# A decoder layer on one core: in its attention stage, the masking and maximum step goes ahead of other work of VectorE

## The chip, the cores and the metric

The kernel runs on one core of one Trainium2 chip, on its own. The metric is the device time of one execution in microseconds (us). Engines are named as in the profile: PE is TensorE (PEld its weight loads), DVE is VectorE, ACT is ScalarE, POOL is GpSimd, and SP is the queue that issues most transfers.

## What is computed

The reference is one layer of a decoder over 512 tokens of width 1024. The input is normalised and projected; one branch pools over windows; the other is a sparse attention with three branches (compressed keys, selected blocks, sliding window) of 16 heads in 2 groups; both are gated, merged and projected, and a squared-ReLU MLP follows. The part that the change touches is the softmax of the selected and the window branch. With 512 tokens there are 8 blocks of 64 keys and up to 16 may be picked, so all causal blocks are picked, and both branches are causal softmaxes over the whole sequence:

```python
def masked_softmax(s, mask):
    s = jnp.where(mask, s.astype(jnp.float32), NEG_INF)
    return jnp.where(mask, jax.nn.softmax(s, axis=-1), 0.0)
...
        s_s = jnp.einsum('bqghd,bgqkd->bghqk', qb, k_sel) * scale
        p_s = masked_softmax(s_s, ok[:, :, None])
        o_s = jnp.einsum('bghqk,bgqkd->bqghd', p_s, v_sel)
...
        s_w = jnp.einsum('bqghd,bkgd->bghqk', qb, kwb) * scale
        p_w = masked_softmax(s_w, wmask)
        o_w = jnp.einsum('bghqk,bkgd->bqghd', p_w, vwb)
        o = gb[..., 0:1] * o_c + gb[..., 1:2] * o_s + gb[..., 2:3] * o_w
```

## The kernel before, in words

Everything is in float32. A weight is split by ACT and DVE into a rounded part and a rest (`wh` on L522, `wl` on L525), and a product is made of three PE products of such parts. The attention stage lies between about 171 and 363 us. Its work is cut into 96 **slots** (`slots`, L1373): 8 pairs of heads, 12 slots to a pair. In the first four slots of a pair (queries 0 to 255) a slot holds both branches, in the other eight (queries 256 to 511) one branch of one head and one block of 128 queries. A slot passes through these steps, each a function:

- `score_pe` (L1387): two PE products (`KH`, `KL`) of 256 to 512 columns into a PSUM bank `psS`. There are three such banks (`S_BANKS`); the scores of the compressed branch, `psC` of `cmp_scores`, take one of the same three at times.
- `smax` (L1408): the step of the change. One DVE instruction for each branch in the slot reads the bank, adds the causal mask, writes the result to a tile `P` in SBUF, and gives each row's extreme to `sm` (a second, short instruction reads the accumulator; the scores are kept negated, so the maximum is taken as a minimum). Once it is done, the bank is free. There are five `P` tiles (`P_BUFS`), so the step of slot i needs the tile of slot i-5, which is free when that slot's transposes are done.
- `expo` (L1425): ACT makes the exponentials in place, with the rows' sums.
- `weight` (L1433): DVE takes reciprocals of the sums (L1440), and POOL multiplies `P` by them and by the gate (L1443).
- `turn_pe`, `turn_hi`, `turn_lo` (L1454, L1469, L1473): PE transposes `P` into a bank `psT` (two of them, `T_BANKS`), ACT copies out the rounded part (L1471) and DVE the rest (L1476). The transposes of slot t need `turn_lo` of slot t-2.
- `pv` (L1478): PE multiplies by the values into the bank `psO`, of which there is one. It begins with two products of the compressed branch (L1485), and these need the bank's last contents taken away by `o_evac` (ACT on L1501, two DVE additions on L1503).

Between these steps PE is given **fillers**: projections of later use (`fill`, `psF` on L566). DVE also splits their weights (L525), does the softmax of the compressed branch (`cmp_scores`, L1336 to L1348) and the rotation of the queries (L905, L948, L949).

The loop at L1518 writes the steps down slot by slot: score of slot i+1, transposes of slot i-4, then `smax` and `expo` of slot i, `weight` of slot i-1, `turn_lo` of slot i-4, and `pv` two slots later (`LAG`, `PLAG`). This is not the order on the engines. A scheduler works through the program as it is built and gives each engine its next instruction by a priority, which by default is the place in the written program; it also gives out the buffers. `tc.high_priority(n)` moves what is written under it n places ahead in this ranking. The order and the buffers are fixed once the program is built, and each engine works through its own list.

Of the kernel before, what the change touches and what calls it, by code (L numbers as in the profile page):

```python
# [62 lines left out]
def trunk(ctx: ExitStack, tc: tile.TileContext, A, out):  # L63
# [519 lines left out]
    def step_side():  # L583
        for _ in range(len(side)):
            g = side.popleft()
            try:
                next(g)
                side.append(g)
            except StopIteration:
                pass  # L590
# [362 lines left out]
    with ExitStack() as c1:  # L953
# [261 lines left out]
        for k in P1[2:]:  # L1215
            i = int(k[-1]) if k[-1].isdigit() else None
# [51 lines left out]
    with ExitStack() as c2:  # L1268
# [46 lines left out]
        def fill(n=1):  # L1315
            for _ in range(n):
                if next(filler, True):
                    return False
                fdone[0] += 1
            return True  # L1320
# [66 lines left out]
        def score_pe(i):  # L1387
            p, half, br, qb, h = slots[i]
            g = p // 4
            nb = qb + 1  # L1390
            ps = ps2.tile([128, S], F32, tag="S", bufs=S_BANKS, name="psS")
            q = Q[p][:, h, 128 * qb:128 * qb + 128]
            for K, a in ((KH[g], True), (KL[g], False)):
                if half == 0:
                    rhs, n = K[:, 0:nb, :, :], 256 * nb
                else:
                    rhs, n = K[:, 0:nb, br, :], 128 * nb
                PE.matmul(ps[:, 0:n], q, rhs, start=a, stop=not a, skip_group_check=True)  # L1398
            live[i] = ps

        def blocks(i):
            p, half, br, qb, h = slots[i]
            nb = qb + 1
            if half == 0:
                return [(b, 128 * nb * b, nb) for b in range(2)]
            return [(br, 0, nb)]

        def smax(i):  # L1408
            p, half, br, qb, h = slots[i]
            ps = live[i]  # L1410
            sm = p2.tile([128, 3, 2], F32, tag="sm", bufs=6, name="sm")
            P = p2.tile([128, S], F32, tag="P", bufs=P_BUFS, name="P")
            for e, (b, o, nb) in enumerate(blocks(i)):
                n = 128 * nb
                if half == 0:
                    s = ps[:, 0:2 * n].rearrange("p (a b c) -> p a b c", b=2, c=128)[:, :, b, :]
                else:
                    s = ps[:, 0:n].rearrange("p (a c) -> p a c", c=128)
                m = cmask[:, S - n:].rearrange("p (a c) -> p a c", c=128)
                DVE.tensor_tensor_reduce(out=P[:, o:o + n].rearrange("p (a c) -> p a c", c=128), in0=s, in1=m,  # L1420
                                         scale=1.0, scalar=3e38, op0=ALU.add, op1=ALU.min,
                                         accum_out=sm[:, 0, e:e + 1])
            live[i] = (ps, sm, P)
# [30 lines left out]
        def turn_pe(i):  # L1454
            p, half, br, qb, h = slots[i]
            ps, sm, P = live[i]
            n = sum(b[2] for b in blocks(i))
            pt = ps2.tile([128, S], F32, tag="T", bufs=T_BANKS, name="psT")
            for j in range(n):
                PE.transpose(pt[:, 128 * j:128 * j + 128], P[:, 128 * j:128 * j + 128], ident)  # L1460
            live[i] = (pt, n)
# [7 lines left out]
        def turn_hi(i):  # L1469
            src, dH, dL = turn_views(i)  # L1470
            his.append(ACT.activation(dH, src, AF.Copy))  # L1471
# [46 lines left out]
        for i in range(n + LAG + PLAG):  # L1518
            if i < n:
                p = slots[i][0]  # L1520
                if i % 12 == 3 and p + 1 < NPAIR:
                    while p + 1 not in Q:
                        fill()
                        step_side()
                if i % 12 == CMP_AT and p + 1 < NPAIR:
                    side.append(cmp_scores(p + 1))
            if i + 1 < n:
                score_pe(i + 1)
                scored["pairs"] = (i + 2) // 12
            t = i - LAG  # L1530
            if 0 <= t < n:
                turn_pe(t)
                turn_hi(t)
            if i < n:
                smax(i)
                expo(i)
            if 0 <= i - 1 < n:
                last = weight(i - 1)
                slot.update(long=i > 3 and slots[i - 1][1] == 1, scaled=last)
            if i > 7 and i % 12 in (0, 2, 4) and len(begun) > 2:  # L1540
                add_sum(last)
            if 0 <= t < n:
                slot["low"] = turn_lo(t)
            step_side()
            want = done0 + (total - done0) * (i + 1) // (n + LAG + PLAG)
            while fdone[0] < want and fill():
                pass
            if i < 5:
                fill()
            if turning:  # L1550
                turn_c()
            j = t - PLAG
            if 0 <= j < n and j % 2 == 1 and pv(j):
                o_evac(*slots[j][0:2])
# [614 lines left out]
```

## Time and profile before

| | |
|---|---|
| time, median of 3 runs | 764.82 us (764.74 to 765.19) |
| profiled execution: its time | 764.3 us |
| its span, first to last instruction | 762.5 us |
| granted clock of TensorE, mean | 0.997 of full speed |
| attention stage, from the timeline | about 171 to 363 us |

The times are of whole executions; the rows of the trace come from the one profiled execution and count from the start of its span. In the timeline a row gives the start, the length, the engine, the line of the kernel, the operation and its tiles, and in square brackets how long the engine was idle just before and what ended that. Buffer numbers are left out there, so a slot is told by its place in the row of slots. Busy time of PE includes the time for which a product's columns run through the array after the next one has begun.

### The profile page before, as it was taken

What the parts mean: (1) busy time and instruction counts of PE and PEld (TensorE: products, weight loads), DVE (VectorE), ACT (ScalarE), POOL (GpSimd) and SP (SyncE); (2) the same over time, 40 slices, a digit from 0 to 9 for tenths busy, and PEclk for the clock granted to TensorE, in tenths of its full rate; (3) what the DMA queues carried; (4) which work ended last, traced back from release to release, by engine and by line L of the source; (5) the groups of instructions that cost most, each with busy time, mean ns of one, the idle gap of its engine ahead of it and who ended that gap; (6) DMA issues with size and microseconds to landing.
All of it is one profiled execution on the core that took longest, in us unless ns stands there. A gap on an engine that the chain in (4) does not pass through costs nothing.

```text
span 762.5 us, 13262 instructions
## 1 busy us (share of the span) xinstructions
PE 752.3 (99%) x4661; PEld 669.7 (88%) x4661; DVE 671.2 (88%) x1282; ACT 513.9 (67%) x978; POOL 190.9 (25%) x271
## 2 busy tenths in 40 slices
PE   9999999999999999999999999999999999999996
PEld 7889999888888888888888899989998999899985
DVE  7998999549988889989689999998899788978897
ACT  7677655339878888898746576944774477447754
POOL 4101010017857767566000020111111111110002
PEclk9999999999999999999999999999999999999998
DMA  9769886864675847343684699989998999798632
GB/s 302 218 187 269 244 239 153 223 188 128 104 195 147 185 106 152 56 112 65 160 294 127 204 289 264 287 218 331 295 267 214 317 299 264 220 302 251 196 110 110
DMA packets 120572, 158.09 MB, mean 207 GB/s; under 512 B 6037, under 2 KB 88505, under 8 KB 120250
## 3 DMA queue, kind: packets, MB, share of 16 engines
q1 hardware_dynamic: 98346, 127.62, 51.5%
q0 software_dynamic: 21872, 28.84, 24.1%
q10 hardware_dynamic: 288, 0.79, 0.4%
q8 instruction: 37, 0.61, 0.3%
q14 instruction: 29, 0.24, 0.1%
HBM read 152.50 MB, written 59.77 MB: 278 GB/s over the span
## 4 chain that ended last, share of the span: by engine, by line
PE 91%; DVE 6%; ACT 2%; issue 1%; DMA 1%; POOL 0%; DVEq 0%; POOLq 0%
PE psB L1705 22%; PE psB L640 21%; PE psF L566 19%; PE psV L640 5%; PE psB L566 4%; PE psS L1398 4%; PE psO L1494 4%; PE psT L1460 4%; PE psV L566 2%; PE psF L704 2%; PE psC L1015 1%; DVE P L1420 1%; DVE PT L1476 1%; PE psT L566 1%; PE psC L1329 1%
## 5 line engine op out<-in xcount | busy, mean ns | idle before, releaser
L396 ACT ACTIVATE wh<-raw 128x1024 fp32r<-128x1024 f32 x72 | 76.0, 1058 | 75.1 <-PE psB L640 28.1
L566 PE MATMUL psF<-R,wh 128*128 128x512 f32 x384 | 124.6, 400 | 0.0
L349 POOL DMA_DIRECT2D S<-w_ff x44 | 49.1, 1128 | 299.8 <-DMA S<-w_ff 238.3
L1443 POOL TENSOR_SCALAR P<-P,sm,GT 128x128 f32<-128x128 f32 (+3 forms) x128 | 89.7, 786 | 60.6 <-DVE sm L1440 29.4
L402 DVE TENSOR_TENSOR wl<-raw,wh 128x1024 fp32r<-128x1024 f32 x72 | 87.8, 1222 | 10.3 <-ACT wh L396 9.7
L566 PEld LDWEIGHTS psF<-R,wh 128*128 128x128 f32 x384 | 68.8, 188 | 11.3
L1430 ACT ACTIVATE P<-P,sm 128x128 f32<-128x128 f32 (+3 forms) x128 | 71.0, 557 | 10.3 <-DVE sm L1420 6.8
L566 PE MATMUL psF<-R,wl 128*128 128x512 f32 x192 | 75.5, 393 | 0.0
L522 ACT ACTIVATE wh<-raw 128x512 fp32r<-128x512 f32 (+1 forms) x76 | 45.1, 616 | 29.3 <-PE psF L566 20.8
L1420 DVE CUSTOM_DVE_ANT_0 P<-psS,cst 128x128 f32<-128x128 f32 (+3 forms) x128 | 59.4, 483 | 4.9 <-PE psT L1460 2.7
L396 ACT ACTIVATE w3h<-raw 128x1024 fp32r<-128x1024 f32 x36 | 38.1, 1058 | 36.3 <-PE psB L640 14.7
L525 DVE TENSOR_TENSOR wl<-raw,wh 128x512 fp32r<-128x512 f32 (+1 forms) x74 | 51.6, 711 | 10.7 <-ACT wh L522 10.3
L1471 ACT ACTIVATE PT<-psT 128x512 fp32r<-128x512 f32 (+2 forms) x96 | 48.9, 520 | 13.7 <-PE psT L1460 12.6
L1476 DVE TENSOR_TENSOR PT<-psT,PT 128x512 fp32r<-128x512 f32 (+2 forms) x96 | 56.2, 592 | 1.5 <-ACT PT L1471 1.3
L1460 PE MATMUL psT<-ident,P 128*128 128x128 f32 x320 | 50.2, 273 | 0.6 <-POOL rx L912 0.3
L402 DVE TENSOR_TENSOR w3l<-raw,w3h 128x1024 fp32r<-128x1024 f32 x36 | 44.0, 1221 | 5.6 <-ACT w3h L396 5.4
L1494 PE MATMUL psO<-PT,VV 128*128 128x256 f32 x320 | 48.5, 286 | 0.0
L1460 PEld LDWEIGHTS psT<-ident,P 128*128 128x128 f32 x320 | 39.5, 140 | 9.4 <-issue 0.8
L640 PE MATMUL psB<-R,wh 128*128 128x256 f32 x336 | 46.3, 279 | 0.0
L1494 PEld LDWEIGHTS psO<-PT,VV 128*128 128x128 f32 x320 | 42.2, 188 | 1.3 <-ACT PT L1471 0.3
L640 PEld LDWEIGHTS psB<-R,wh 128*128 128x128 f32 x336 | 42.5, 188 | 0.2
L566 PEld LDWEIGHTS psF<-R,wl 128*128 128x128 f32 x192 | 36.0, 188 | 7.5
(454 smaller groups left out, 2078.2 us busy)
## 6 DMA issues: line engine op xcount, KB each, us to landing
raw<-w_ff SPq DMA_DIRECT2D x54, 512.0 KB, 5.9
S<-w_ff POOLq DMA_DIRECT2D x44, 512.0 KB, 9.3
raw<-S SPq DMA_DIRECT2D x44, 512.0 KB, 5.5
S<-w_ff SPq DMA_DIRECT2D x32, 512.0 KB, 7.0
raw<-w_in SPq DMA_DIRECT2D x31, 512.0 KB, 5.5
S<-S SPq DMA_DIRECT2D x12, 512.0 KB, 5.6
S_o<-w_out POOLq DMA_DIRECT2D x8, 512.0 KB, 8.0
raw<-w_proj_nsa SPq DMA_DIRECT2D x8, 512.0 KB, 4.2
```

The lines of the kernel that those rows point to most:

```text
L396: ACT.activation(h, t, AF.Copy)
L402: DVE.tensor_tensor(l, t, h.bitcast(F32), op=ALU.subtract)
L525: eng.tensor_tensor(l[:, sl], t[:, sl], h[:, sl].bitcast(F32), op=ALU.subtract)
L566: PE.matmul(ps, a, b, start=first and j == 0, stop=last and j == n - 1, skip_group_check=True)
L640: r = PE.matmul(out, w[u][:, k, 128 * f:128 * f + 128], moving[v][:, k, :], **kw)
L1420: DVE.tensor_tensor_reduce(out=P[:, o:o + n].rearrange("p (a c) -> p a c", c=128), in0=s, in1=m, scale=1.0, scalar=3e38, op0=ALU.add, op1= ...
L1430: last_exp[:] = [ACT.activation(c, c, AF.Exp, bias=sm[:, 0, e:e + 1], scale=-1.0, accum_out=sm[:, 1, e:e + 1])]
L1443: r = POOL.tensor_scalar(P[:, o:o + n], P[:, o:o + n], sm[:, 2, e:e + 1], GT[:, qb, c + e:c + e + 1], op0=ALU.mult, op1=ALU.mult)
L1460: PE.transpose(pt[:, 128 * j:128 * j + 128], P[:, 128 * j:128 * j + 128], ident)
L1476: return DVE.tensor_tensor(dL, src, dH.bitcast(F32), op=ALU.subtract)
L1494: PE.matmul(ps[:, qb % 2, :, :], VV[:, k, b, g, :], t[:, j, :, :], start=False, stop=last and j == len(kbs) - 1 and t is tL, skip_group_ch ...
L1705: PE.matmul(ps[f], self.Y.of(y)[u][:, 2 * g + k, 128 * f:128 * f + 128], w[v][:, k, :], start=first and g == k == u == v == 0, stop=g == k ...
```

## The change

The step that masks and takes the extremes (`smax`) is put under `high_priority(60)`; the exponentials after it are not.

```diff
             if i < n:
-                smax(i)
+                with tc.high_priority(60):
+                    smax(i)
                 expo(i)
```

The instructions are the same, none is added or removed; their order on the engines changes. In the rows below, names carry their numbers. The P tiles of slots 2, 3 and 4 are P_1995, P_2007 and P_2038, those of slots 27 and 28 are P_2714 and P_2764; an `ISA` row with P is the step of the change, the `ISA sm` row is its short second instruction, and the reciprocals of slots 0 and 1 read sm_1973 and sm_1982.

DVE at slots 27 and 28; before:

```order
L1420 ISA P_2714,sm_2713<-psS_2682,cst_136 128x256
L1420 ISA sm_2713 128x1
L1476 TENSOR_TENSOR PT_2691<-psT_2685,PT_2690 128x4x128
L525 TENSOR_TENSOR wl47_2745<-raw43_1932,wh47_2744 128x512
L1476 TENSOR_TENSOR PT_2691<-psT_2707,PT_2690 128x4x128
L1336 TENSOR_TENSOR cw_2732<-psC_2723,cst_136 128x8x32
L1420 ISA P_2764,sm_2763<-psS_2704,cst_136 128x384
L1420 ISA sm_2763 128x1
```

and after:

```order
L1420 ISA P_2714,sm_2713<-psS_2682,cst_136 128x256
L1420 ISA sm_2713 128x1
L1420 ISA P_2764,sm_2763<-psS_2704,cst_136 128x384
L1420 ISA sm_2763 128x1
L1476 TENSOR_TENSOR PT_2691<-psT_2685,PT_2690 128x4x128
L525 TENSOR_TENSOR wl47_2745<-raw43_1932,wh47_2744 128x512
L1476 TENSOR_TENSOR PT_2691<-psT_2707,PT_2690 128x4x128
L1336 TENSOR_TENSOR cw_2732<-psC_2723,cst_136 128x8x32
L1440 RECIPROCAL sm_2713<-sm_2713 128x2
```

The step of slot 28 moves from behind two `turn_lo` (of slots 22 and 23), a weight split and L1336 to the place right behind the step of slot 27.

PE where the bank `psO` is begun again (psO_2960), from the transposes of slot 31 on (P_2841); psF_2990 is a filler. Before:

```order
L1460 MATMUL psT_2945<-ident_61,P_2841 128x128 x4
L1398 MATMUL psS_2969<-KH0_137,Q_2177 128x256
L1398 MATMUL psS_2969<-KL0_139,Q_2177 128x256
L566 MATMUL psF_2990<-R1_64,wh47_2744 128x512
L1485 MATMUL psO_2960<-pc_2672,VC00_145 128x2x128
L1485 MATMUL psO_2960<-pc_2672,VC01_146 128x2x128
L1494 MATMUL psO_2960<-PT_2869,VV_141 128x256
```

and after:

```order
L1460 MATMUL psT_2945<-ident_61,P_2841 128x128 x4
L1398 MATMUL psS_2969<-KH0_137,Q_2177 128x256
L1398 MATMUL psS_2969<-KL0_139,Q_2177 128x256
L566 MATMUL psF_2990<-R1_64,wh47_2744 128x512
L566 MATMUL psF_2990<-R2_65,wh47_2744 128x512
L566 MATMUL psF_2990<-R1_64,wl47_2745 128x512
L566 MATMUL psF_2990<-R1_64,wh47_2744 128x512
L566 MATMUL psF_2990<-R2_65,wh47_2744 128x512
L566 MATMUL psF_2990<-R1_64,wl47_2745 128x512
L1398 MATMUL psS_3001<-KH0_137,Q_2177 128x512
L1485 MATMUL psO_2960<-pc_2672,VC00_145 128x2x128
L1485 MATMUL psO_2960<-pc_2672,VC01_146 128x2x128
```

Six fillers stand ahead of the first product into psO instead of one, and the first product of slot 38's score (psS_3001) stands there too. On DVE the steps of slots 35 and 36 have moved ahead of the two additions of L1503 that empty the bank; before, both stood behind them.

DVE at the first slots of the stage; before:

```order
L1420 ISA P_1995,sm_1994<-psS_1979,cst_136 128x256
L1420 ISA sm_1994 128x1
L1440 RECIPROCAL sm_1973<-sm_1973 128x2
L1420 ISA P_2007,sm_2006<-psS_1991,cst_136 128x256
L1420 ISA sm_2006 128x1
L1420 ISA P_2007,sm_2006<-psS_1991,cst_136 128x256
L1420 ISA sm_2006 128x1
L1440 RECIPROCAL sm_1982<-sm_1982 128x2
L1420 ISA P_2038,sm_2037<-psS_2003,cst_136 128x384
L1420 ISA sm_2037 128x1
```

and after:

```order
L1420 ISA P_1995,sm_1994<-psS_1979,cst_136 128x256
L1420 ISA sm_1994 128x1
L1420 ISA P_2007,sm_2006<-psS_1991,cst_136 128x256
L1420 ISA sm_2006 128x1
L1420 ISA P_2007,sm_2006<-psS_1991,cst_136 128x256
L1420 ISA sm_2006 128x1
L1420 ISA P_2038,sm_2037<-psS_2003,cst_136 128x384
L1420 ISA sm_2037 128x1
L1440 RECIPROCAL sm_1973<-sm_1973 128x2
L1440 RECIPROCAL sm_1982<-sm_1982 128x2
```

The steps of slots 3 and 4 move ahead of the reciprocals of slots 0 and 1.

## Rows read from the trace of the kernel before

**Rows 1.** The page's first part: busy time, share of the span and instructions.
```profile
PE 752.3 (99%) x4661; PEld 669.7 (88%) x4661; DVE 671.2 (88%) x1282; ACT 513.9 (67%) x978; POOL 190.9 (25%) x271
```
**Rows 2.** The attention stage as one stretch: us, then busy time (count) by engine, granted clock, DMA.
```profile
171.00:363.00 192.00, 190.13 (x1230) 167.23 (x1229) 173.84 (x579) 163.66 (x445) 132.13 (x195) 1.00 0.57 126
```
**Rows 3.** Waits of PE and POOL in that stretch: total us, times, longest.
```profile
PE psS L1398 <- DVE sm L1420: 0.9, 2, 0.6
PE psO L1485 <- DVE oT L1503: 0.4, 1, 0.4
PE psT L1460 <- POOL rx L912: 0.3, 1, 0.3
PE psT L1460 <- DVE PT L1476: 0.2, 1, 0.2
...
POOL P L1443 <- DVE sm L1440: 29.4, 25, 3.0
```
**Rows 4.** Timeline (start, us, work, [idle before]) of PE and DVE around slot 30.
```profile
224.15 0.38 PE L1460 MATMUL psT<-ident,P 128*128 128x128 f32 x2
225.10 0.47 PE L1398 MATMUL psS<-KH,Q 128*128 128x512 f32 x1 [0.57 <-DVE sm L1420]
...
222.27 0.68 DVE L1476 TENSOR_TENSOR PT<-psT,PT 128x512 fp32r<-128x512 f32 x1
222.87 0.68 DVE L525 TENSOR_TENSOR wl<-raw,wh 128x512 fp32r<-128x512 f32 x1
223.47 0.68 DVE L1476 TENSOR_TENSOR PT<-psT,PT 128x512 fp32r<-128x512 f32 x1
224.07 0.41 DVE L1336 TENSOR_TENSOR cw<-psC,cst 128x256 f32<-128x256 f32 x1
224.40 0.54 DVE L1420 CUSTOM_DVE_ANT_0 P<-psS,cst 128x384 f32<-128x384 f32 x1
224.88 0.08 DVE L1420 DVE_READ_ACCUMULATOR2_ANT sm<- 128x1 f32 x1
```
**Rows 5.** Chain of work that ended last, in the stage: six filler products.
```profile
252.28 1.39 PE psF L566 x6
```
**Rows 6.** Timeline around the start of a psO accumulation: PE, then DVE.
```profile
236.88 0.60 PE L1460 MATMUL psT<-ident,P 128*128 128x128 f32 x4
...
237.55 0.40 PE L566 MATMUL psF<-R,wh 128*128 128x512 f32 x1
238.35 0.47 PE L1485 MATMUL psO<-pc,VC 128*128 128x256 f32 x2 [0.40 <-DVE oT L1503]
...
237.37 0.84 DVE L1503 TENSOR_TENSOR oT<-psO,ot 64x256 f32<-64x256 f32 x2
```
**Rows 7.** Timeline around slot 50's transposes: PE, then DVE.
```profile
273.98 0.63 PE L1460 MATMUL psT<-ident,P 128*128 128x128 f32 x4 [0.15 <-DVE PT L1476]
...
273.42 0.41 DVE L1476 TENSOR_TENSOR PT<-psT,PT 128x256 fp32r<-128x256 f32 x1
```
**Rows 8.** Timeline around slot 66's transposes: PE, then DVE.
```profile
306.38 0.63 PE L1460 MATMUL psT<-ident,P 128*128 128x128 f32 x4 [0.34 <-POOL rx L912]
...
305.69 0.55 DVE L1476 TENSOR_TENSOR PT<-psT,PT 128x384 fp32r<-128x384 f32 x1
```
**Rows 9.** Timeline at slot 15's score: PE.
```profile
191.93 0.50 PE L1398 MATMUL psS<-KH,Q 128*128 128x512 f32 x1 [0.34 <-DVE sm L1420]
```
**Rows 10.** Timeline of the stage's first slots: DVE, POOL, PE.
```profile
174.38 0.17 DVE L1440 RECIPROCAL sm<-sm 128x2 f32<-128x2 f32 x1
174.47 0.40 DVE L1420 CUSTOM_DVE_ANT_0 P<-psS,cst 128x256 f32<-128x256 f32 x1
...
175.15 0.17 DVE L1440 RECIPROCAL sm<-sm 128x2 f32<-128x2 f32 x1
...
174.72 1.74 POOL L1443 TENSOR_SCALAR P<-P,sm,GT 128x128 f32<-128x128 f32 x4 [7.37 <-PE psS L1398]
...
176.91 0.38 PE L1460 MATMUL psT<-ident,P 128*128 128x128 f32 x2
```

## The prediction

> **What bounds the kernel now.** I read the page's first part, then the stretch in which the change acts, then the waits in it, and then each wait of PE in the timeline. PE is busy for 752.3 of 762.5 us [rows 1]; no other engine comes near. In the attention stage, 192 us long, PE is busy for 190.13 us, at the full granted clock (1.00), and DVE for 173.84 us [rows 2]. So the stage is as long as PE's own work, and since the change neither adds nor removes a PE product, it can only give or cost time where PE stands and waits. Those waits are short and few: 0.9 us in two places for the step that is moved (a score waits for its bank), 0.4 us in one for the additions that empty psO, 0.3 and 0.2 us in one each in front of transposes [rows 3], 1.8 us in brackets together.
>
> A bracket understates what a wait costs, because a product's modelled end lies behind the point at which the next one could have begun. Two transposes take 0.38 us and four take 0.60 or so [rows 4, 6], so a further one costs 0.11; after the pair at 224.15 PE was free again at 224.37, and not at 224.53. Each wait therefore costs its bracket and about 0.16 us more. The five waits cost 0.73 us at 225.10 [rows 4], 0.56 at 238.35 [rows 6], 0.31 at 273.98 [rows 7], 0.50 at 306.38 [rows 8] and 0.50 at 191.93 [rows 9], 2.6 us in all, 0.34% of the kernel. That is about the ceiling of what this change can give; below it there is only a tenth or two at some products that wait for a copy, which I leave at zero.
>
> **The change, place by place.** The step goes ahead of other work on DVE. So banks come free earlier and exponentials start earlier; whatever the step overtakes (turn_lo, reciprocals, weight splits, the additions of L1503) stands later on DVE by the length of the step: the distance from one start to the next is 0.48 us with 384 columns (224.40 to 224.88) [rows 4]. I price it at the five waits and at the one place where I find a new wait.
>
> *Slot 30's score, 225.10.* It waits for the step of slot 28, which stands behind four other DVE instructions, from 222.27 to 224.40, and ends its first part at 224.88 [rows 4]. In the new order it stands at their head. It would run at about 222.27, the bank would be free some 2.1 us earlier, and the wait goes: -0.73. What is late next is the two turn_lo that it overtook. They move by 0.48, to 222.75 and 223.95, and end by 224.63. The transposes of slots 24 and 25 need them; the first stand at 224.15 with the first turn_lo done at 223.43, and the second would stand after slot 30's score, near 224.9. No new wait, with 0.3 us to spare.
>
> *The psO bank, 238.35.* It waits for the additions of L1503, which run at 237.37 for 0.84 us [rows 6]. In the new order two steps stand ahead of them, and the second needs the transposes of slot 31, which end at 237.48 [rows 6]. If it starts there and takes at most the 0.48 of a 384-column step (its two halves have 128 columns each), the additions end near 238.8. PE, though, now has five more fillers in front, and six fillers take 1.39 us in the chain [rows 5], 0.23 each; with the first product of slot 38's score that makes 1.39 us more of work. Free at 237.55 + 0.23 = 237.78, it comes to psO at 239.17. So the wait goes, with a spare of 0.37 us; that DVE's queue may also be held by other things there makes me count -0.4 of the 0.56, with 0 and -0.56 as ends.
>
> *Slot 50's transposes, 273.98.* They wait for the turn_lo of slot 48, done at 273.83 [rows 7]. In the new order the steps of slots 53 and 54 (384 and 512 columns) go ahead of it, about 1.1 us, so it would be done at 274.9. PE has moved two scores and two fillers in front of the transposes, about 0.8 + 0.46 us, and comes to them near 274.9 as well. I count -0.25, between 0 and -0.31.
>
> *Slot 66's transposes, 306.38.* They wait for the turn_lo of slot 64, done at 306.24 [rows 8], behind a weight split. The step of slot 70 goes ahead of it, but the steps before that have moved too, so that it comes at about the same time; what helps is that two fillers (0.46 us) now stand before the transposes. -0.45, between 0 and -0.5.
>
> *Slot 15's score, 191.93.* In the new order it takes another of the three banks and no longer waits for the step of slot 12: -0.5.
>
> *The first slots, 174 to 177.* Here the order costs. The reciprocals of slots 0 and 1 stood at 174.38 and 175.15; POOL, idle until then, did its four multiplications from 174.72 to 176.46, and the transposes of slot 1 followed at 176.91 [rows 10]. In the new order the steps of slots 3 (0.68 us, from 174.47 to 175.15) and 4 (0.48) stand in front. The first reciprocal comes at about 174.38 + 0.68 + 0.48 = 175.5, the multiplications run to about 177.6, and the second transpose of slot 1 begins near 177.75 and not at 177.02 (the second of the pair at 176.91). PE has nothing else in front of it to do: +0.7. The least is 0, if PE finds work there; the most is the whole shift of the reciprocals, +1.15.
>
> The sum: -0.73 - 0.4 - 0.25 - 0.45 - 0.5 + 0.7 = -1.6 us. From the profiled execution's 764.3 us (span 762.5) that gives 762.7; on the median of the three runs, 764.82, which is 0.5 above it, 763.2. With every term at its better end it is -2.6, so 762.2, and 761.5 if some of the smaller waits go too; with the uncertain terms at their worse ends it is -0.73 - 0.5 + 1.15 = -0.1, so 764.7.
>
> The queues: the transfers of the rotation (L895) move behind one weight load and one transfer of a sum on SP at one place, and POOL's order changes only around the compressed branch. POOL does not wait for a transfer anywhere in the rows of its waits that I went by; it waits for reciprocals, 29.4 us [rows 3], so I price both at nothing. If that cover were gone, POOL would hold the multiplications, and with them the transposes.
>
> A rule speaks against the change. At both scores PE waited for a bank. The Trainium skill (Perfetto Trace Analysis, Optimization Strategy) says that the same gap coming again and again on the engine that should be saturated can mean that there is not enough room for the next tile, a matter of the count of buffers. If that were all of it here, another order on DVE would leave the bank waits as they are, the sum would lose 1.2 us, and the time would be 764.4. The trace agrees only in part: the bank is indeed what lacks, but it lay waiting for DVE for over 2 us behind four instructions that nobody needed yet [rows 4].
>
> **The rivals.** *The waits come back at the next step (no change).* Each turn_lo, reciprocal and split that is overtaken is late by about 0.5 to 1.1 us, and the spare that I found is 0.3 to 0.4 us at two places and nothing at a third. If half of the 2.3 us of gains is given back, 1.2 us, the sum is -0.4 and the time 764.4. For it speaks that DVE is busy for 91% of the stage; against it, that PE's fillers were moved with the waits, so that it has other work where the new order makes a producer late.
>
> *Reciprocals held behind the step (slower).* The step needs the P tile of five slots before, so it can stand at the head of DVE's queue and wait for transposes, and behind it stand the reciprocals that POOL needs for the next transposes. In the order before, the last reciprocal ahead of a slot's step is that of slot i-3 or later in all 96 places; in the new one it is slot i-4 or older in 13. If 13 places cost half of what I found at the first slots, 0.35 us each, that is 4.5 us; with the sum of -1.6 the time is 764.82 + 2.9 = 767.8. It decides where a slot's multiplications end less than about 1 us before its transposes. For it: POOL's waits are mostly for reciprocals [rows 3]. Against it: such waits stand before POOL, and only those that reach PE cost anything; among PE's waits no such row comes near the size of the others [rows 3].
>
> *The change does nothing* can't be: the order moves at most slots; only its effect may be nil, and that is the first rival.
>
> **How the numbers follow.** Two tenths of a per cent, 1.5 us, is about what a measurement of this kernel can tell from no change. My forecast, a gain of 0.8 to 3 us, has a chance of 0.57; 763.2 lies at its middle and just beyond that bound, and its larger part, 0.46, lies on the faster side. The first rival has 0.25, and with the smaller part of the forecast that makes 0.36 for the same. The second rival has 0.18. The range of 761.4 to 766.6 goes from the best end of the terms to a part of the second rival; about 0.07 is left out below it and 0.13 above.
>
> **What would show it.** Right: PE's waits for the moved step gone from the stage's waits; the row after the pair of transposes near 224 without a bracket; slot 1's transposes about 0.7 us later than 176.9; PE's busy time the same, and the span shorter by about 1.6. Wrong: brackets of PE that name L1443 or L1476, or DVE waiting longer in front of L1420 for PE's transposes, with reciprocals behind it; then the second rival holds. If the bank waits stay, the first term was misread.

## The result

The changed kernel takes 769.31 us (median of 6 runs, 768.88 to 769.57) beside 764.78 us of the kernel before (6 runs, 764.44 to 765.20): a ratio of 1.0059, 95% interval 1.0048 to 1.0069. It is slower by 4.5 us, where 763.2 was forecast and 766.6 was the end of the range. The profiled execution took 769.57 us, with a span of 767.7.

The profile after, in the views that were shown of before. First the page's first part, which answers to [rows 1]; then the attention stage as one stretch, five microseconds longer than in [rows 2], so that it ends at about the same work; then the waits of PE and POOL in the stage, which answer to [rows 3] (total us, times, longest).

```profile
PE 754.7 (98%) x4661; PEld 669.5 (87%) x4661; DVE 672.6 (88%) x1282; ACT 515.2 (67%) x978; POOL 191.5 (25%) x271
```

```profile
171.00:368.00 197.00, 192.92 (x1231) 167.03 (x1230) 175.37 (x579) 164.89 (x444) 132.65 (x195) 1.00 0.57 125
```

```profile
PE psO L1485 <- ACT PT L1471: 1.2, 1, 1.2
PE psT L1368 <- DVE sm L1440: 0.7, 1, 0.7
PE psT L1460 <- DVE PT L1476: 0.6, 2, 0.4
PE psO L1485 <- DVE oT L1503: 0.4, 1, 0.4
PE psS L1398 <- DVE sm L1420: 0.3, 1, 0.3
PE psT L1460 <- POOL P L1443: 0.3, 1, 0.3
```

```profile
POOL P L1443 <- DVE sm L1440: 34.0, 18, 6.3
```

```profile
DVE P L1420 <- PE psT L1460: 5.9, 13, 0.8
```

The granted clock is the same and so is the work. PE's busy time is 2.8 us more in a window that is 5 us longer, because part of every wait is counted as busy time, as the prediction read it from the brackets; its idle time went from 1.9 to 4.1 us. What has changed is the places where PE stands. The two waits for the moved step (0.9 us in [rows 3]) have shrunk to one of 0.3. In their place stand a start of psO (1.2; the row names ACT's copy of L1471, which ended 0.07 us before, but the second addition of L1503 ended 0.15 before, as at the other starts of psO that wait, and the first product needs it and not the copy), the compressed branch's transposes (L1368, 0.7) and transposes that wait for turn_lo. POOL waits 34.0 us for reciprocals where it waited 29.4 [rows 3], and DVE stands 5.9 us ahead of the moved step, for PE's transposes to free a P tile, where in the kernel before it stood 2.7:

```profile
DVE P L1420 <- PE psT L1460: 2.7, 8, 0.8
```

Brackets don't add up to the loss, so I set the same product of both traces side by side: how much later it ends in the changed kernel. Each row of this table is a place, and each column one trace less the trace of before; the last three columns are the first three experiments. The stage starts up to 1 us earlier or later in every execution, whatever the order of DVE, so only the differences down a column count.

| end of | after | early | middle | late |
|---|---|---|---|---|
| slot 0's score (172.2 before) | +0.4 | +0.2 | -0.1 | +0.3 |
| slot 29's score (224.3) | +2.2 | +2.05 | -0.05 | +0.4 |
| slot 30's score (225.8) | +1.4 | +2.05 | -0.85 | +0.35 |
| slot 33's score (232.5) | +2.1 | +2.05 | -0.15 | +0.35 |
| slot 62's score (288.1) | +2.1 | +2.15 | -0.2 | +0.35 |
| slot 64's score (292.4) | +2.9 | +2.15 | +0.6 | +0.4 |
| slot 92's score (346.9) | +3.35 | +2.15 | +1.0 | +0.4 |
| slot 93's score (349.8) | +4.85 | +2.15 | +1.0 | +1.85 |
| slot 95's transposes (360.9) | +5.2 | +2.2 | +1.05 | +2.2 |

So 1.8 us are lost in the first slots, 0.8 gained at slot 30, 0.7 lost right behind it, 0.8 at 291, 0.4 more by slot 76, 1.5 at 350 and 0.4 at the end: 4.8 us in the stage.

A second count doesn't depend on which product stands where. It takes the distance from each product's start to the next one's and subtracts what is usual for a product of that width (0.23 us with 512 columns, 0.18 with 384, 0.12 with 256, 0.11 for a transpose). What is left over the stage is 3.7 us before and 8.6 after, 4.9 more. Where a single wait is given below "by spacing", it is this figure; the prediction's prices of the five waits (0.73, 0.56, 0.31, 0.50, 0.50) are the same within 0.01.

*Slot 30* goes as forecast. The step of slot 28 (384 columns) now runs at 224.53, ahead of a turn_lo, and PE's pair of transposes at 226.37 is followed by the score with no bracket, where [rows 4] has 0.57:

```profile
224.53 0.55 DVE L1420 CUSTOM_DVE_ANT_0 P<-psS,cst 128x384 f32<-128x384 f32 x1
...
225.01 0.68 DVE L1476 TENSOR_TENSOR PT<-psT,PT 128x512 fp32r<-128x512 f32 x1
...
226.37 0.38 PE L1460 MATMUL psT<-ident,P 128*128 128x128 f32 x2
...
226.51 0.47 PE L1398 MATMUL psS<-KH,Q 128*128 128x512 f32 x1
```

*psO near 231* is where that gain is given back. The timeline of after first, then the same place before:

```profile
231.19 0.42 DVE L1503 TENSOR_TENSOR oT<-psO,ot 64x256 f32<-64x256 f32 x1
...
231.53 0.68 DVE L1420 CUSTOM_DVE_ANT_0 P<-psS,cst 128x512 f32<-128x512 f32 x1
...
232.14 0.55 DVE L1420 CUSTOM_DVE_ANT_0 P<-psS,cst 128x384 f32<-128x384 f32 x1
...
232.72 0.42 DVE L1503 TENSOR_TENSOR oT<-psO,ot 64x256 f32<-64x256 f32 x1
...
233.29 0.48 PE L1485 MATMUL psO<-pc,VC 128*128 128x256 f32 x2 [0.44 <-DVE oT L1503]
```

```profile
230.00 0.84 DVE L1503 TENSOR_TENSOR oT<-psO,ot 64x256 f32<-64x256 f32 x2
...
231.25 0.40 PE L1485 MATMUL psO<-pc,VC 128*128 128x256 f32 x2
```

Before, both additions ended at 230.84 and PE came to psO at 231.25: no wait, but only 0.41 us to spare. The steps of slots 31 and 32 now stand between the two halves of the additions, 1.2 us of DVE, and PE waits.

### The profile page after: what moved, and what is told of

It reads as the page before. It is cut to its first block, busy times and chain, and to the rows that moved or that the text cites. A ratio compares the mean times of both kernels' runs of the same rounds, so it can differ in the third digit from the quotient of the medians.

```text
span 767.7 us, 13288 instructions
## 1 busy us (share of the span) xinstructions
PE 754.7 (98%) x4661; PEld 669.5 (87%) x4661; DVE 672.6 (88%) x1282; ACT 515.2 (67%) x978; POOL 191.5 (25%) x271
## 4 chain that ended last, share of the span: by engine, by line
PE 88%; DVE 7%; ACT 2%; issue 1%; POOL 1%; DMA 1%; DVEq 0%; POOLq 0%
PE psB L1706 22%; PE psB L640 20%; PE psF L566 17%; PE psV L640 5%; PE psB L566 4%; PE psS L1398 4%; PE psO L1494 4%; PE psT L1460 4%; PE psV L566 2%; DVE P L1420 2%; PE psF L704 2%; PE psC L1015 1%; DVE PT L1476 1%; ACT P L1430 1%; PE psT L566 1%
## 5 line engine op out<-in xcount | busy, mean ns | idle before, releaser
L1443 POOL TENSOR_SCALAR P<-P,sm,GT 128x128 f32<-128x128 f32 (+3 forms) x128 | 94.2, 857 | 62.3 <-DVE sm L1440 34.0
L1420 DVE CUSTOM_DVE_ANT_0 P<-psS,cst 128x128 f32<-128x128 f32 (+3 forms) x128 | 59.1, 486 | 9.3 <-PE psT L1460 5.9
L1471 ACT ACTIVATE PT<-psT 128x512 fp32r<-128x512 f32 (+2 forms) x96 | 49.3, 522 | 18.6 <-PE psT L1460 17.4
L1476 DVE TENSOR_TENSOR PT<-psT,PT 128x512 fp32r<-128x512 f32 (+2 forms) x96 | 55.8, 590 | 1.4 <-ACT PT L1471 1.1
```

The source lines that it names most:

```text
L1443: r = POOL.tensor_scalar(P[:, o:o + n], P[:, o:o + n], sm[:, 2, e:e + 1], GT[:, qb, c + e:c + e + 1], op0=ALU.mult, op1=ALU.mult)
L1476: return DVE.tensor_tensor(dL, src, dH.bitcast(F32), op=ALU.subtract)
```

## The experiments

Every edit below is made in the changed kernel unless it says otherwise. Times are medians; ratios are to runs of the kernel before on the same chip. `nullcontext()` leaves a step at its default place.

**Theory A**, formed from the waits of after: the step stands at the head of DVE's queue and waits there for its P tile; whatever is behind it comes late. **Theory B** is the slower rival of the prediction, reciprocals held behind the step, at 13 places. **Theory C** is plain overtaking: on a DVE that is nearly always busy each step put ahead delays the rest by its own length, and it costs where that rest empties the bank that PE wants next. The first three runs cut the change in three.

*early.*
```diff
-                with tc.high_priority(60):
+                with tc.high_priority(60) if i < 24 else nullcontext():
```


> The priority is given only to the steps of slots 0 to 23; from slot 24 on the order is that of the kernel before. Theory A (the step stands at the head of VectorE's queue and waits there for its P tile; whatever stands behind it comes late, and PE pays where it needs that next): by the shift between the two traces the first 24 slots lose 1.8 us (0.4 at slot 0, 2.2 at slot 20), so about 766.6. Theory B (only the reciprocals that stand behind a step are what is late): 8 of the 13 places with a reciprocal of four slots before lie here; their share of the 4.5 us is 2.8 us, 767.6. Theory C (the first slots as I priced them, 0.7 us of loss, and 0.5 gained at slot 15): 765.0.


Measured 766.44 us beside 764.63, ratio 1.0024 (1.0015 to 1.0033).

*middle.*
```diff
+                with tc.high_priority(60) if 24 <= i < 86 else nullcontext():
```


> The priority is given only to the steps of slots 24 to 85. Theory A: slot 30's score gains 0.8, and PE loses 0.7 at the first product into psO near 234 us, where one of the two additions stands behind a step, 0.8 at the transposes of the compressed branch near 293 us and 0.4 near 310 to 319 us; in sum 1.1 us slower, 765.9. Theory B: 5 of the 13 places lie here, 1.7 us, less slot 30's 0.8: 765.7. If both of the gains that I had forecast stand (slot 30 and psO at 238 us) and nothing else: 763.7.


Measured 765.69, ratio 1.0017 (1.0008 to 1.0025).

*late.*
```diff
+                with tc.high_priority(60) if i >= 86 else nullcontext():
```


> The priority is given only to the steps of slots 86 to 95; VectorE's order from there to the end is word for word that of the changed kernel, and before it that of the kernel before. Theory A: PE waits at the first product into psO near 353 us, because the second of the two additions that empty it stands behind the step of slot 92, which waits for the transposes of slot 87 to free its P tile: 1.5 us there and 0.4 at the end, 766.6 (as 764.8 + 1.9). Theory B: no reciprocal is four slots behind its step here, so nothing, 764.8.


Measured 766.48, ratio 1.0024 (1.0015 to 1.0033).

The three losses, 1.8, 1.1 and 1.85 us, add up to 4.7, the loss of the whole (4.5) within what these medians tell. So the thirds lose independently of each other. That theory A's times came out shows no more than this, since they had been read off the shifts between before and after; and in middle A (765.9) and B (765.7) can't be told apart by the time. Theory B falls as the cause of all: late has none of its 13 places and loses as much as early, which has 8. But the trace of late also contradicts the account that I had given of it, that the step of slot 92 waits for its P tile. In the timeline of late, DVE does not stand ahead of that step:

```profile
345.71 1.83 POOL L1443 TENSOR_SCALAR P<-P,sm,GT 128x384 f32<-128x384 f32 x2
...
345.92 2.58 DVE L1303 TENSOR_TENSOR R<-oT,R 128x256 fp32r<-128x256 f32 x3
...
348.43 0.68 DVE L1420 CUSTOM_DVE_ANT_0 P<-psS,cst 128x512 f32<-128x512 f32 x1
...
349.04 0.41 DVE L1503 TENSOR_TENSOR oT<-psO,ot 64x256 f32<-64x256 f32 x1
...
349.37 0.54 DVE L1420 CUSTOM_DVE_ANT_0 P<-psS,cst 128x384 f32<-128x384 f32 x1
...
349.95 0.42 DVE L1503 TENSOR_TENSOR oT<-psO,ot 64x256 f32<-64x256 f32 x1
...
350.51 0.36 PE L1485 MATMUL psO<-pc,VC 128*128 128x256 f32 x1 [1.22 <-ACT PT L1471]
```

The time came out right for a wrong reason. What is odd here is the second row: three splits of 0.41 us take 2.58. (A merged row shows the shape of its first instruction; of POOL's two multiplications the second, of slot 90, has 512 columns.)

*three_slots.*
```diff
+                with tc.high_priority(60) if 26 <= i <= 28 else nullcontext():
```


> The priority is given only to the steps of slots 26, 27 and 28, so that slot 28's goes ahead of a turn_lo, two splits and another turn_lo; VectorE's order is that of the kernel before but for small shifts up to slot 46. Theory A: slot 30's score no longer waits, and nothing else is late: 0.7 to 0.8 us faster, 764.0. Rival (a wait taken away comes back at the next step that was overtaken): 764.8, with a bracket of 0.3 to 0.7 at the transposes of slots 24 or 25 or at psO behind them.


Measured 764.02, ratio 0.9995 (0.9981 to 1.0009); from slot 29 to slot 30 the scores shift by -0.8 and 0.14 of it is given back by slot 38. The first term of the prediction, the wait at slot 30, is real and is had alone; by itself it is too small for this measurement.

*late_additions_first.*
```diff
+                with tc.high_priority(60) if i >= 86 else nullcontext():
                     smax(i)
...
+                with tc.high_priority(60):
                     DVE.tensor_tensor(oT[p // 4][64 * h:64 * h + 64, p % 4, 256 * half:256 * half + 256].rearrange(
...
```


> As the run called late (priority for the steps of slots 86 to 95), and the additions of L1503 have the same priority: both now stand ahead of the steps of slots 91 and 92, and ahead of slot 95's; the rest of VectorE's order from slot 86 on stays (before it, only the additions pass a rotation step, a reciprocal or a split at a few places). In the trace of late the step of slot 92 began with no idle time before it, so my account of a wait for its P tile can't be right there; VectorE was full of splits (L1303) until 348.5 us. Theory C (plain overtaking: the second addition comes two steps, 1.2 us, later on a full VectorE, and psO is the one bank that PE needs next): the waits of 1.46 and 0.2 us at psO go, 764.8. Rival D (the loss lies in PE's own order, where half of a score now stands ahead of psO): nothing changes, 766.5.


Measured 766.53, ratio 1.0030 (1.0018 to 1.0042). By the products, 0.75 us are lost before slot 30, where the additions pass something else, and 1.55 from slot 93 on (1.85 in late): nearly all of it is still there, though both additions stand ahead of the steps. Around psO PE's order is back to that of before, so rival D falls; but theory C in my form, that the loss hangs on the additions, falls too. The timeline of this run:

```profile
348.48 0.84 DVE L1504 TENSOR_TENSOR oT<-psO,ot 64x256 f32<-64x256 f32 x2
...
349.35 0.69 DVE L1420 CUSTOM_DVE_ANT_0 P<-psS,cst 128x512 f32<-128x512 f32 x1
...
349.97 0.55 DVE L1420 CUSTOM_DVE_ANT_0 P<-psS,cst 128x384 f32<-128x384 f32 x1
...
350.45 1.28 DVE L1476 TENSOR_TENSOR PT<-psT,PT 128x512 fp32r<-128x512 f32 x2
...
349.47 0.48 PE L1485 MATMUL psO<-pc,VC 128*128 128x256 f32 x2 [0.29 <-DVE oT L1504]
...
351.28 0.52 PE L1460 MATMUL psT<-ident,P 128*128 128x128 f32 x3 [0.51 <-DVE PT L1476]
```

PE waits less at psO and then for the psT bank, which the two turn_lo empty; these now stand behind additions and steps. DVE as a whole is late, since the splits end at 348.56 here too, and the order behind them only chooses who waits.

*early_not_3_4.*
```diff
+                with tc.high_priority(60) if i < 24 and i not in (3, 4) else nullcontext():
```


> As the run called early (priority for the steps of slots 0 to 23), but not for slots 3 and 4, so that the reciprocals of slots 0 and 1 again stand ahead of those two steps; from slot 5 on VectorE's order is the same as in early. If the loss of the first slots is that POOL gets these reciprocals late, the waits of 0.21, 0.52 and 0.32 us at the transposes of slots 0 and 1 go: 766.4 - 1.05 = 765.4. If it is made up of all the reciprocals that stand behind steps up to slot 20, two of eight places go: 766.0.


Measured 765.16, ratio 1.0013 (1.0004 to 1.0022). Of early's 1.8 us the reciprocals of slots 0 and 1 make 1.1, as the first theory has it. In early:

```profile
175.67 0.22 DVE L1440 RECIPROCAL sm<-sm 128x2 f32<-128x2 f32 x2
...
176.00 3.25 POOL L1443 TENSOR_SCALAR P<-P,sm,GT 128x128 f32<-128x128 f32 x6 [8.40 <-issue]
...
177.80 0.76 PE L1460 MATMUL psT<-ident,P 128*128 128x128 f32 x2 [0.30 <-POOL P L1443]
...
178.60 0.69 DVE L1420 CUSTOM_DVE_ANT_0 P<-psS,cst 128x512 f32<-128x512 f32 x1 [0.70 <-PE psT L1460]
```

POOL starts at 176.00 and not at 174.72 [rows 10], PE waits for it with slot 1's transposes, and DVE then stands for these transposes, with the next reciprocals behind the step that waits: theories A and B both, in this one place. The other 0.7 us of early lie between slots 16 and 25 in small waits that I didn't take apart further.

*all_additions_first.* The second edit of late_additions_first, with the priority of the changed kernel for all slots.


> The changed kernel, with the additions of L1503 given the same priority. Theory C: PE's waits at psO go, 0.7 us near 231, 1.5 near 351 and some 0.2 near 359; the early ones and the transposes of the compressed branch stay late: 769.3 - 2.4 = 766.9. If the waits come back at the steps that are now behind the additions: 769.


Measured 770.74, ratio 1.0089 (1.0075 to 1.0102), slower than the changed kernel. The waits at psO shrink, and others grow: by the same comparison of products, the compressed branch's transposes near 291 (before's time) lose 1.15 us (0.8 in after), and the first 30 slots 3.2 (1.8 in after). So that the additions are overtaken is not the cause by itself; turn_lo or the reciprocals alone were not tried.

*all_steps_first.*
```diff
+                with tc.high_priority(60):
                     smax(i)
+            with tc.high_priority(60):
                 DVE.reciprocal(sm[:, 2, 0:nb_], sm[:, 1, 0:nb_])
+            with tc.high_priority(60):
                 return DVE.tensor_tensor(dL, src, dH.bitcast(F32), op=ALU.subtract)
+                with tc.high_priority(60):
                     DVE.tensor_tensor(oT[p // 4][64 * h:64 * h + 64, p % 4, 256 * half:256 * half + 256].rearrange(
...
```


> The changed kernel, with the same priority for the additions of L1503, the reciprocals of L1440 and turn_lo (L1476): the four kinds keep their order among each other nearly as before, and only weight splits, the rotation and the compressed branch's steps are overtaken. Theory C (what costs is that steps of the attention itself are overtaken): slot 30's wait goes (its step passes a split and L1336), the new waits don't appear: 764.0. Rival E (the overtaken side work then comes late: the rotated queries of the next pair, or the compressed branch's transposes): 766, with PE waiting at a score or at L1368.


Measured 763.31, ratio 0.9988 (0.9979 to 0.9997): 1.2 us faster than the kernel before by the medians, and 6.0 faster than the changed one. In the stage it gains 0.8, all of it at slot 30; the other 0.4 lies within the interval and has no place in the stage. Of the new waits of after only that of L1368 is there, at another place. PE's waits in the stage (in this kernel's lines, L1487 is the first product into psO and L1461 the transposes):

```profile
PE psT L1368 <- POOL P L1444: 0.5, 1, 0.5
PE psO L1487 <- ACT wh L522: 0.4, 1, 0.4
PE psT L1461 <- ACT pc L1370: 0.2, 1, 0.2
```

The order among the four kinds is not quite that of before: 80 pairs of their rows on DVE stand the other way round, where after has 236, and the moved step passes one of the other three 37 times, where it does so 199 times in after. With that, passing the splits and the rotation costs nothing that shows, and the loss is gone whole. So what costs in the changed kernel comes of one of the four passing the other three. One run that moves all of them at once doesn't tell how much each kind has in it.

**The late loss.** One row was still unexplained, the splits of 2.58 us. **Theory P**: such a split reads two operands from SBUF and stands still while GpSimd multiplies. In late the reciprocals of slots 89 and 90 both come before four of the splits, and POOL runs their two multiplications back to back, from 345.71. Two runs take the two halves of late apart.

*late_86_to_90.*
```diff
+                with tc.high_priority(60) if 86 <= i <= 90 else nullcontext():
```


> Priority for the steps of slots 86 to 90 only. On VectorE the reciprocal of slot 90 stands ahead of four splits (L1303), as in the run called late, but both additions stand ahead of the steps of slots 91 and 92, as in the kernel before. Theory P (in late one split of L1303 took 1.91 us and not 0.42, from 345.92 to 347.83, exactly over two multiplications of GpSimd that stood back to back because both reciprocals had come early; a split that reads two operands from SBUF stands still while GpSimd works): the long split is here too, the additions end 1.4 us later and PE, which had 0.8 us to spare at psO, waits some 0.6 us: 765.2. Theory C (only that the additions stand behind two steps): no loss, 764.6, whatever the split takes.


Measured 765.42, ratio 1.0019 (1.0005 to 1.0033).

*late_91_to_95.*
```diff
+                with tc.high_priority(60) if i >= 91 else nullcontext():
```


> Priority for the steps of slots 91 to 95 only: the second addition stands behind the steps of slots 91 and 92, as in late, but the reciprocal of slot 90 stands behind four of the splits, as in the kernel before. Theory P and C together (each costs its own delay, less the 0.8 us that PE has to spare at psO): no long split, the additions 1.2 us later, a wait of 0.4 us at psO and the 0.4 us of the end: 765.4. Theory C alone for the whole loss: 1.5 and 0.4, 766.5. If the split is the whole cause: 764.9.


Measured 765.12, ratio 1.0008 (0.9999 to 1.0017): by the time alone not to be told from no change, but the place can be read. The stage loses 0.7 us, 0.24 of it waiting at psO.

*late_86_to_90_cut.* As late_86_to_90, and in `weight`:
```diff
-                n = 128 * nb
+                n = 8 if i in (89, 90) else 128 * nb
```


> As the run called late_86_to_90, and GpSimd's multiplications of slots 89 and 90 cover 8 of their 384 columns (the other columns stay unscaled, so these two slots' part of the output is not the reference's); the order on every engine is the same. In late_86_to_90 one split took 1.91 us, from 345.10 to 347.01, over these two multiplications (344.89 to 346.73), and PE then waited 0.53 us at psO and 0.7 near 358. Theory P (the split stands still because GpSimd works): every split takes 0.4 to 0.5, the additions come 1.5 us earlier and the wait at psO goes: about 0.5 to 0.9 less, 764.5 to 764.9. If the split is long for another reason (its operands, ScalarE's half of the split): 1.9 us again, and 765.4.


Measured 764.40, ratio 0.9998 (0.9989 to 1.0007). Of the two multiplications the first has 384 columns and the second 512; both were cut to 8. In late_86_to_90 the stage loses 1.1 us, 0.44 of it waiting at psO and most of the rest at transposes near 357.5, which I didn't take apart; here it loses nothing. The two intervals just overlap, so the rows have to decide:

```profile
345.70 1.42 DVE L1303 TENSOR_TENSOR R<-oT,R 128x256 fp32r<-128x256 f32 x4
345.82 1.66 POOL L1443 TENSOR_SCALAR P<-P,sm,GT 128x8 f32<-128x8 f32 x2
```

In late_86_to_90 these four splits take 2.92 us. POOL's two rows stand beside them in the cut too, and nearly as long (1.66 us, where late_86_to_90 has 1.84); what is gone is most of what they read and write.

The rows of the 16 splits of L1303 (duration in ns: least, median, longest) of before, late, late_86_to_90, late_91_to_95 and the cut, in this order:

```profile
L1303 DVE TENSOR_TENSOR R<-oT,R x16: 400/416/794, 341.8 to 367.2; 128x256 fp32r<-128x256 f32 x16
```
```profile
L1303 DVE TENSOR_TENSOR R<-oT,R x16: 403/416/1910, 342.2 to 369.4; 128x256 fp32r<-128x256 f32 x16
```
```profile
L1303 DVE TENSOR_TENSOR R<-oT,R x16: 405/412/1911, 341.4 to 367.9; 128x256 fp32r<-128x256 f32 x16
```
```profile
L1303 DVE TENSOR_TENSOR R<-oT,R x16: 401/417/789, 343.0 to 369.0; 128x256 fp32r<-128x256 f32 x16
```
```profile
L1303 DVE TENSOR_TENSOR R<-oT,R x16: 406/415/451, 342.4 to 367.6; 128x256 fp32r<-128x256 f32 x16
```

The long split comes with the early reciprocal (1.91 us in late and in late_86_to_90) and goes when POOL's multiplications are cut to 8 columns (0.45 at most, with the order on every engine the same as that of late_86_to_90). PE's wait at psO, by spacing, is 1.38 us in late, 0.44 with the long split alone, 0.24 with the overtaken addition alone, and none in the cut. This is what a spare of 0.8 us gives. Before, the additions ended at 347.75 and PE came to psO at 348.57,

```profile
346.91 0.84 DVE L1503 TENSOR_TENSOR oT<-psO,ot 64x256 f32<-64x256 f32 x2
...
348.57 0.40 PE L1485 MATMUL psO<-pc,VC 128*128 128x256 f32 x2
```

and since PE begins about 0.15 us after the end of the additions where it waits for them (349.95 + 0.42 and 350.51 in late), the usable part of the spare is 0.67. Counted from slot 92's score, the additions end 1.1 us later with the long split alone (before has one split of 0.79, so the long one adds 1.1 and not 1.5), 1.1 with the overtaking alone and 2.2 with both. With the split alone, 1.1 less 0.67 leaves the 0.44. In the other two half a score stands ahead of psO, 0.18 us of work more: 0.27 and 1.4, where 0.24 and 1.38 were measured. Each delay alone has to use up the spare first, and both together use it up once. In this place theory P and theory C hold together, C in the plain form that the additions come late on a full DVE, by whatever stands ahead of them; A and B don't.

*middle_less_seven.*
```diff
+                with tc.high_priority(60) if 24 <= i < 86 and i not in (31, 32, 61, 62, 63, 67, 68) else nullcontext():
```


> As the run called middle (priority for the steps of slots 24 to 85), but not for slots 31 and 32, 61 to 63, 67 and 68. The additions then stand ahead of the steps of 31 and 32, and the copies that empty psT for the compressed branch's transposes (turn_lo of slot 58) come as early as in the kernel before. Theory C (a step costs where what it overtakes is what empties the bank that PE wants next): the waits of 0.7 us near 231, 0.8 near 291 and about 0.3 near 307 go, slot 30's gain stays: 765.7 - 1.8 = 763.9. If such waits only move on: 765 or more.


Measured 763.92, ratio 0.9999 (0.9989 to 1.0009): 1.8 us less than middle by the medians, 1.5 against the runs of before that each was compared with. By the products within the stage it is 1.15: the loss of 0.7 near 231 is gone whole, that of 0.4 between 307 and 319 too, and slot 30's 0.8 stays; but of the 0.8 at L1368 only 0.15 is had back. So the place near 231 is shown to be the two steps. For L1368 the trace of after shows that the turn_lo that empties the bank (of slot 56, by the count of transposes) ends at 292.97, 0.14 us before PE goes on:

```profile
292.43 0.54 DVE L1476 TENSOR_TENSOR PT<-psT,PT 128x384 fp32r<-128x384 f32 x1
...
292.95 0.54 DVE L1476 TENSOR_TENSOR PT<-psT,PT 128x384 fp32r<-128x384 f32 x1
293.11 0.51 PE L1368 MATMUL psT<-identR,PC 128*128 128x128 f32 x4 [0.65 <-DVE sm L1440]
```

In the kernel before the same turn_lo ended at 289.43 and PE came at 289.59, without a wait and with next to nothing to spare:

```profile
288.88 0.55 DVE L1476 TENSOR_TENSOR PT<-psT,PT 128x384 fp32r<-128x384 f32 x1
...
289.59 0.50 PE L1368 MATMUL psT<-identR,PC 128*128 128x128 f32 x4
```

In middle_less_seven it ends at 289.02, 0.41 us earlier than before; but PE, with the gains of slot 30 and psO, comes there 1.0 us earlier and waits 0.60:

```profile
288.47 0.55 DVE L1476 TENSOR_TENSOR PT<-psT,PT 128x384 fp32r<-128x384 f32 x1
...
289.17 0.51 PE L1368 MATMUL psT<-identR,PC 128*128 128x128 f32 x4 [0.45 <-DVE sm L1440]
```

So at this place the other case of the expectation holds: what PE has gained is given back where DVE is not as far ahead. Which of the steps ahead of that turn_lo make it late in after stays open.

## Why the prediction was wrong

*The bound* was read rightly: PE's work and its clock are unchanged, and the whole effect lies in PE's waits (4.9 us by spacing, 4.8 of the stage). But "no other engine comes near" passes over DVE, which the prediction itself has at 91% of the stage: it is full enough that a step put ahead makes the rest late.

*Slot 30* (-0.73 forecast): -0.8 in after, -0.8 in three_slots and in all_steps_first. Right in place, size and mechanism. The rule of the Trainium skill that was weighed there (Perfetto Trace Analysis, Optimization Strategy), by which the wait could speak of too few banks, is not borne out: with the same three banks the order alone takes it away.

*psO at 238.35* (-0.4): by spacing the wait shrinks from 0.57 to 0.15 us, as forecast, and small waits at the transposes behind it (0.16 and 0.24) take the 0.4 back. *Slots 50, 66 and 15* (-0.25, -0.45, -0.5): no gain. Slot 50's wait is gone, but by slot 60 the scores are as late as they were ahead of it; slot 66's is as long as before (0.50 before, 0.56 after); slot 15's is gone and slot 16's score waits 0.48 in its place. For these four the first rival was right: the wait comes back at the next step.

*The first slots* (+0.7): 1.1 by early against early_not_3_4. Mechanism and place right; the size was too small, though within the 1.15 that was named as the most.

*The step that failed* is the sentence "I price it at the five waits and at the one place where I find a new wait", and with it the sum. A list of the waits of before can only show what may be gained. The losses stand where PE did *not* wait before but had little to spare: 0.41 us at psO near 231 (lost 0.7), 0.16 at L1368 near 290 (0.8), 0.82 at psO near 349 (1.5), and small ones at slots 16 to 25, between 307 and 319 and at the end (0.7, 0.4 and 0.4). The prediction had the tool: it set the additions against PE's arrival at 238.35. It did so at one of the starts of psO, the one with a bracket, and not at the others.

*The slower rival* had the right side and, at 767.8, nearly the time, for a mechanism that accounts for about a quarter of the loss. Its price, 0.35 us at each of 13 places, is not what the runs show: two of the places make 1.1 us, and the late third loses 1.85 us without one. Its argument "such waits stand before POOL, and only those that reach PE cost anything; among PE's waits no such row comes near the size of the others" reads the waits of the old order to judge the new one. The signs that were named for it did come (brackets of PE that name L1443 and L1476, DVE waiting 5.9 us and not 2.7 in front of L1420), and yet it is not the main cause: the plain lateness of turn_lo and the additions shows the same brackets.

*The queues* (nothing): wrong for POOL, in a way that the sentence on it did not consider. POOL was not held up by the change in the late slots. The multiplication of slot 90 started earlier, at 346.53 in late and at 346.83 in before, though late's stage began 0.3 us later; it stood right behind that of slot 89, and the two held DVE.

## What to carry over

When work is given priority on a nearly full in-order engine, price what it overtakes and not only what it releases: for each bank that the overtaken work empties, take from the old trace the time between its end and the moment when the next user comes, and subtract the length of what is put ahead; a small spare with no wait in the profile is where the loss will be. If a priority is wanted, try giving it to all steps of the same chain, so that mostly unrelated work is passed; here that was the one order for the whole stage that lost nothing (all_steps_first). And a step that comes early starts its followers early too: look at what those will run beside.

## What the runs showed of the hardware

A VectorE instruction with two operands in SBUF can stand still while GpSimd multiplies. The split of L1303 takes 0.41 us, 0.79 at the longest with one multiplication beside it (before) and 1.91 with two back to back; with these two cut to 8 columns it takes 0.45 at most. In late and in late_86_to_90 it was not let in between the two. Standing side by side on record is not enough: in before two splits of 0.42 us lie whole within the row of one multiplication (345.06 to 346.31), and only the third takes 0.79. The same shows in the rows of another line of before: L905, with two operands in SBUF, has long outliers, the additions of L1503, which read one from PSUM, have none, though multiplications stand beside many of them (ns: least, median, longest):

```profile
L905 DVE TENSOR_TENSOR rx<-rx,rs x20: 411/418/819, 36.6 to 310.7; 128x256 f32<-128x256 f32 x20
```
```profile
L1503 DVE TENSOR_TENSOR oT<-psO,ot x32: 406/417/421, 185.5 to 366.2; 64x256 f32<-64x256 f32 x32
```

The Trainium skill (SBUF — State Buffer, SBUF: two separate sides) states an exclusive lock between GpSimd instructions that read SBUF and VectorE instructions with two SBUF inputs, held for a whole instruction, with the other side fully blocked. The traces agree (0.79 and 1.91 us where 0.41 is usual), and add that the split stood through two GpSimd instructions in a row.
